# Moving the recurrence's steps and the activation blocks to other places of a fixed matmul stream

## The chip, the cores and the metric

The kernel runs on one core of one Trainium2 chip. The metric is device time in microseconds (us) of the whole program, lower is better. A core has a tensor engine (PE, with its weight loads listed as PEld), a vector engine (DVE), a scalar engine (ACT), a general engine (POOL) and a queue engine that mostly starts transfers (SP). Each executes its own list of instructions in order and waits on semaphores for the others.

## The reference, cut to what matters

One transformer-like block over 256 tokens of width 2048, all in float32:

```python
z = u @ w_in                                   # u = rms_norm(x); z is split eight ways
hq, hf, hi, hg, aq, ak, av, gates = split(z)
g = lb + (1 - lb) * sigmoid(hf); q = silu(hq) * 128**-0.5
o = hgrn2_scan(q, 1 - g, hi, log(g))           # S_t = diag(g_t) S_{t-1} + k_t v_t^T ; o_t = S_t^T q_t
y_a = rms_norm(o) * silu(hg)                   # 8 heads of 128
y_b = chunk_band_attention(aq, ak, av)         # 16 heads of 64, relative bias
merged = sig(gate_a) * (y_a @ w_branch_a) + sig(gate_b) * (y_b @ w_branch_b)
h = x + merged @ w_out
out = rms_norm(h + relu(rms_norm(h) @ w_up)**2 @ w_down)
```

## The kernel before, in words

**Products.** Every float32 product is made of three (or, transposed, two) products of split operands: a weight piece `raw` arrives by a transfer, ACT copies it into a rounded high part `wh`, DVE subtracts to get the low part `wl` (`split`, lines 88 to 90), and PE multiplies high by high, high by low and low by high. One piece is 128 x 1024. `gemm` (lines 143 to 145) spends six products of 128 x 512 on a k tile of 128 rows; `gemm_t` (lines 184 and 185) spends two pairs, each a product of 128 x 256 and one of 128 x 512. PE does little else, so its list is a stream of such products in which the rest of the work must find its place.

**The recurrence.** The scan is not run step by step. For a pair of heads, `hgrn_scores` builds a matrix of decayed scores in five steps: `diagonal` and the factors of level 2; level 2 and the factors of 8; level 8 and the factors of 32; level 32 and the factors of 128; level 128. A level step has eight short float32 products (rows named `ps`, lines 372, 416 and 448), and on DVE some exponents, products (`el`, `er`, `kl`, `qr`) and masked copies into `sd` (lines 374 and 423) that free the two `ps` buffers. `hgrn_out` then has two `outputs` steps (rows `po`, lines 476 and 477: scores times values, then a root mean square that goes ACT, DVE, POOL, DVE, ending in `o`, line 487) and two `finish` steps (rows `tpo`, line 494: transposes, then a split into `act_ya`). Four pairs of heads: pairs 0 and 1 form group 0, pairs 2 and 3 form group 1.

**What sets their order.** The steps wait in a list, `behind`. Each has a gap; `tick` takes 1 from the head's gap at each k tile of `gemm_t`, and 2 at each of `gemm`, and issues the head's step when it reaches zero. `scores(n, a, gap, first)` puts in the five score steps of pair n, `group` the eight output and finish steps of a group. The stream under them is: `hi0`, `hg0`, `hf2`, `hq2`, `hf3`, `hq3` (the input of pair 3 is `a3 = fq(3)`), `hi1`, `hg1`, `aq00`, `aq01`. What is left in the list after `aq01` is issued at once (`while behind: tick(9)`); then the pools of the stage are closed, the attention's tiles are opened in their room, and `ak00` starts. It needs the accumulator that `aq00` held, so `aq00T` (line 193) must have been read out of it; `aq00T` lies in the room of the recurrence's tiles.

**The second half.** `w_out`, `w_up` and `w_down` are done as `Unit`s: two column blocks at once, of which the first half of the k tiles uses a scheme with seven products of sums (`A`, `B`, `C`, `D`, left operands `S2`, `S4`, `S5`, `S7` that are sums of activation blocks, built by `combos`) and the second half plain products (`plain`). A unit has slots: `u.step(next(at))` is called at eleven places of `run`, numbered from 0, and issues one of the unit's waiting steps if the slot's number is at least `start`. Slot 0 lies ahead of the product `12 C`, slot 1 ahead of `11 D`, slot 2 ahead of the first plain product, slot 7 after `less("22", u2)`, the one behind the second shared copy `u2`. Besides, `plain` first issues every waiting step whose number is at most the block that it needs: at k tiles 8 and 9 that is block 2. `h_blocks` and `turns` make the steps: transposes of a block of activations (rows `tp_h`, `tp_u`, line 106), a scaling on DVE for `h` (`hw`, line 981), a split into `act_h` or `act_u`. Unit `up00` issues `h_blocks(2)`, the `dn` units whose name ends in 0 issue `turns(2)`; `wo2` issues `h_blocks(0)` and the sums of `h`; `up02`, `up12` and so on issue `turns(0)` and the sums of `u`.

The program's scheduler orders each engine's list after that, by priority and by its own notion of readiness; weight splits have high priority.

Of the kernel before, what the change touches and what calls it, by code (L numbers as in the profile page):

```python
# [50 lines left out]
def tile_hybrid_block(  # L51
# [107 lines left out]
    def later(*steps):  # L159
        behind.extend([n, f] for n, f in steps)  # L160
# [45 lines left out]
    steps = [1, 1] + [2] * (KD // 2 - 1)  # L206
# [11 lines left out]
    for kt, n in zip(starts, steps):  # L218
        c, a = kt // 4, kt % 4
        xw = h2(f"xw{kt}")[:, :n]  # L220
        nc.sync.dma_start(xw, x_t[:, kt:kt + n, :])
        with tc.high_priority(offset=2000):
            for j in range(n):
                g, hi = wmix[:, kt + j:kt + j + 1], xT[c][:, a + j, 0, :]
# [62 lines left out]
    f0, z0 = h2("f0"), h2("zq0")  # L287
# [11 lines left out]
    f1, z1 = h2("f1"), h2("zq1")  # L299
# [212 lines left out]
    def scores(n, a, gap, first=None):  # L512
        sc, steps = hgrn_scores(n, *a)
        later(*[(gap if i or first is None else first, f) for i, f in enumerate(steps)])
        return sc

    def group(g, s0, s1, vs, gws, gap):
        o0, f0 = hgrn_out(g, 0, s0, vs, gws)
        o1, f1 = hgrn_out(g, 2, s1, vs, gws)
        later(*[(gap, f) for f in o0 + o1 + f0 + f1])  # L520

    ya += [new_act(f"ya{g}") for g in range(2)]
    a0, a1 = fq(0), fq(1)
    s0 = scores(0, a0, 7, 14)
    vs0 = v_chunk(0)
    s1 = scores(1, a1, 7)
    gws0 = hg_chunk(0)
    a2 = fq(2)
    group(0, s0, s1, vs0, gws0, 4)
    a3 = fq(3)  # L530
    s2 = scores(2, a2, 7)
    vs1 = v_chunk(1)
    s3 = scores(3, a3, 7)
    gws1 = hg_chunk(1)
    group(1, s2, s3, vs1, gws1, 4)
    acc_q = [gemm_t(xT, w_in_t, C_AQ + i * T, KD, f"aq0{i}") for i in range(2)]
    while behind:
        tick(9)
# [60 lines left out]
    for g in range(2):  # L599
# [3 lines left out]
        vs = []  # L603
# [6 lines left out]
        for pr in range(5):  # L610
            last = pts
# [18 lines left out]
    def combos(lhs, what, home, made, blocks=None):  # L630

        a = {}

        def block(m, j):
            if blocks:
                a[m, j] = blocks[m, j]
                return
            a[m, j] = fours(token(f"a{m}{j}_{what}"))
            x = lhs[j][:, :, :, m * P:(m + 1) * P].bitcast(F32)
            nc.vector.tensor_tensor(a[m, j], x[:, :, 0, :], x[:, :, 1, :], op=ALU.add)  # L640

        def final(i, s):
            t = home.tile([P, 4, 2, P], F32R, name=f"S{i}_{what}", tag=f"S{i}", bufs=1)
            split(t[:, :, 0, :], t[:, :, 1, :], s)
            made[i] = [[t[:, k, u, :] for u in range(2)] for k in range(4)]

        def one():
            for m in range(NM):
                for j in range(2):
                    block(m, j)  # L650
            nc.vector.tensor_tensor(a[1, 1], a[1, 0], a[1, 1], op=ALU.subtract)
            final(5, a[1, 1])

        def two():
            nc.vector.tensor_tensor(a[1, 0], a[0, 0], a[1, 0], op=ALU.subtract)
            nc.vector.tensor_tensor(a[0, 0], a[1, 1], a[0, 0], op=ALU.subtract)
            nc.vector.tensor_tensor(a[0, 1], a[0, 1], a[0, 0], op=ALU.add)
            final(4, a[0, 1])

        return [one, two, lambda: final(2, a[0, 0]), lambda: final(7, a[1, 0])]  # L660
# [69 lines left out]
    class Unit:  # L730
# [78 lines left out]
            return half  # L809

        def step(self, at):
            if at >= self.start and self.steps:
                self.steps.pop(0)[1]()

        def end(self, n):
# [153 lines left out]
    hT = []  # L969
    Sh = {}  # L970

    def h_blocks(n0):

        def one(n, m):
            if not m:
                hT.append(new_act(f"h{n}"))
            hi, lo = hT[n][:, :, 0, :], hT[n][:, :, 1, :]
            t = h1[n][m]
            tp = transpose4(t, f"h{n}{m}")
            tmp = fours(token(f"hw_{n}_{m}"))  # L980
            nc.vector.tensor_tensor(tmp, tp, bc(wmlp[:, 4 * n:4 * n + 4], 2, P), op=ALU.mult)
            split(hi[:, :, m * P:(m + 1) * P], lo[:, :, m * P:(m + 1) * P], tmp)
            nc.scalar.activation(token(f"hsq_{n}_{m}"), t, AF.Square, accum_out=ssq2[:, m, n:n + 1])

        def factor():
            ssum2 = small.tile([P, NM], F32, name="ssum2", tag="ssum")
            nc.vector.tensor_reduce(ssum2, ssq2, axis=AX.X, op=ALU.add)
            rsqrt(rstd2, ssum2, D, NM)

        return [(n, lambda n=n, m=m: one(n, m)) for n in (n0, n0 + 1) for m in range(NM)] + [  # L990
            (n0 + 1, f) for f in ([factor] if n0 else combos(hT, "h", sp, Sh))]

    rstd2 = const.tile([P, NM], F32, name="rstd2")

# [15 lines left out]
    for qd in range(NQ):  # L1010
        last = qd == NQ - 1
        uT, rs, Su, blocks = [], {}, {}, {}

        def turns(c0, uT=uT, rs=rs, Su=Su, blocks=blocks, qd=qd):

            def one(c, m):
                if not m:
                    uT.append(new_act(f"u{qd}{c}"))
                hi, lo = uT[c][:, :, 0, :], uT[c][:, :, 1, :]
                tp = transpose4(rs[c, m], f"u{qd}{c}{m}")  # L1020
                if c < 2:
                    blocks[m, c] = fours(token(f"a{m}{c}_u{qd}"))
                    nc.scalar.copy(blocks[m, c], tp)
                split(hi[:, :, m * P:(m + 1) * P], lo[:, :, m * P:(m + 1) * P], tp)

            return [(c, lambda c=c, m=m: one(c, m)) for c in (c0, c0 + 1) for m in range(NM)] + [
                (c0 + 1, f) for f in ([] if c0 else combos(uT, f"u{qd}", tk, Su, blocks))]

        for c in range(0, 4, 2):
            def done(m, n, acc, c=c, rs=rs, qd=qd):  # L1030
                t = token(f"r{qd}{c}{n}{m}")
                with tc.high_priority(offset=2000):
                    nc.scalar.activation(t, acc, AF.Relu, scale=rstd2[:, m:m + 1])
                nc.scalar.activation(t, t, AF.Square)
                rs[c + n, m] = t

            units.append(Unit(lambda: hT, lambda: Sh, w_up, qd * (FF // NQ) + c * NC, f"up{qd}{c}", done,
                              steps=(lambda turns=turns: turns(0)) if c else (lambda: ()) if qd else (lambda: h_blocks(2)), start=3))

        def out_of(m, n, acc, last=last, qd=qd):  # L1040
            if not last:
                t = token(f"y{qd}{n}{m}")
                with tc.high_priority(offset=2000):
                    nc.scalar.copy(t, acc)
                nc.gpsimd.dma_start(hd[n][m], t, accum_op=ALU.add)
                return
            wf = fin["w"]
            r = fin[m][:, n * NC:(n + 1) * NC]
            evict(r, acc)
            nc.scalar.activation(token(f"ysq_{n}_{m}"), r, AF.Square, accum_out=ssq3[:, m, n:n + 1])  # L1050
            if n < 3:
                nc.vector.tensor_tensor(r, r, wf[:, n * NC:(n + 1) * NC], op=ALU.mult)
                return
            nc.vector.tensor_reduce(ssum3[:, m:m + 1], ssq3[:, m, :], axis=AX.X, op=ALU.add)
            rsqrt(rstd3[:, m:m + 1], ssum3[:, m:m + 1], D, 1)
            f = rstd3[:, m:m + 1]
            for i in range(4):
                t = fin[m][:, i * NC:(i + 1) * NC]
                if i == 3:
                    nc.vector.scalar_tensor_tensor(t, t, f, wf[:, i * NC:(i + 1) * NC], op0=ALU.mult, op1=ALU.mult)  # L1060
                elif i == 2:
                    nc.vector.tensor_scalar(t, t, f, None, op0=ALU.mult)
                else:
                    nc.scalar.activation(t, t, AF.Copy, scale=f)
                (nc.sync if i % 2 else nc.scalar).dma_start(out[m * P:(m + 1) * P, i * NC:(i + 1) * NC], t)

        def finals():
            fin["w"] = apool.tile([P, D], F32, name="wf", tag="act")
            nc.gpsimd.dma_start(fin["w"], bass.AP(tensor=norm_final_w.tensor, offset=norm_final_w.offset, ap=[[0, P], [1, D]]))
            for m in range(NM):  # L1070
                fin[m] = apool.tile([P, D], F32, name=f"fin{m}", tag="act")
                for n in range(4):
                    nc.gpsimd.dma_start(fin[m][:, n * NC:(n + 1) * NC], hd[n][m])

        for n0 in (0, 2):
            units.append(Unit(lambda uT=uT: uT, lambda Su=Su: Su, w_down, n0 * NC, f"dn{qd}{n0}",
                              lambda m, n, acc, n0=n0, out_of=out_of: out_of(m, n0 + n, acc), kt0=qd * KD,
                              steps=(lambda: ()) if n0 else (lambda turns=turns, last=last: turns(2) + [(3, finals)] * last),
                              start=1, tail=last and n0 == 2))

    for u, then in zip(units, units[1:] + [None]):
        run(u, then)
# [44 lines left out]
```

## Time and profile before

| | |
|---|---|
| median of 3 runs | 1416.26 us (1415.25 to 1416.26) |
| profiled execution | 1417.17 us, span 1415.4 us, mean granted clock 0.995 |
| PE busy | 1390.2 us (98%) |
| DVE busy | 1119.4 us (79%) |
| ACT busy | 908.4 us (64%) |
| POOL busy | 137.8 us (10%) |

The span runs from the first to the last instruction; the program's time is some 1.8 us longer. Times of rows count from the start of the span. A row of the timeline has its start, its duration, engine, line, operation, and the number of instructions merged in it; a bracket tells how long the engine had been idle and what ended that. Matmuls are pipelined: a product of 128 x 512 is listed with 0.39 us, and the next starts 0.23 us after it.

### The profile page before, as it was taken

To read this page: it belongs to the slowest core of one execution; us is meant where nothing else is said; L and a number is where in the kernel's file an instruction comes from. 1 tells how busy PE (TensorE), PEld (TensorE's weight loads), DVE (VectorE), ACT (ScalarE), POOL (GpSimd) and SP (SyncE) were. 2 spreads that over 40 slices of the span, in tenths; PEclk is the share of its full clock that TensorE was granted. 3 is DMA by queue.
4 is the path that set the end of the run, shared out by engine and by line. 5 is a ranking of instruction groups with operands and counts; after the bars stand their busy time and mean duration, and the time that the engine had idled before them with its cause. 6 is when DMAs were issued, how large, how long until landed. Compare 5 with 4: busy or idle time off the path is not lost.

```text
span 1415.4 us, 18570 instructions
## 1 busy us (share of the span) xinstructions
PE 1390.2 (98%) x6562; PEld 1150.4 (81%) x6562; DVE 1119.4 (79%) x1410; ACT 908.4 (64%) x1170; POOL 137.8 (10%) x220
## 2 busy tenths in 40 slices
PE   9999998999999999999999999999999999999997
PEld 7788887878787888888877888888888888888885
DVE  7897986675657875688998888779878897778885
ACT  6755744464556665445767876677666876668764
POOL 2000001010000000001210001100101001110200
PEclk9999999999999999999999999999999999999998
DMA  9644455455668987558898898988899888998883
GB/s 327 225 154 160 149 166 165 157 174 169 183 223 236 271 240 254 188 179 252 250 286 251 242 275 224 280 272 254 270 288 277 263 228 252 284 299 260 261 246 118
DMA packets 122925, 327.42 MB, mean 231 GB/s; under 512 B 10944, under 2 KB 11712, under 8 KB 122448
## 3 DMA queue, kind: packets, MB, share of 16 engines
q1 hardware_dynamic: 103264, 264.80, 54.7%
q0 software_dynamic: 18416, 59.84, 21.3%
q10 hardware_dynamic: 1152, 1.60, 0.4%
q8 instruction: 51, 0.84, 0.2%
q14 instruction: 42, 0.34, 0.1%
HBM read 271.67 MB, written 10.49 MB: 199 GB/s over the span
## 4 chain that ended last, share of the span: by engine, by line
PE 88%; DVE 4%; DMA 3%; issue 2%; ACT 2%; POOL 0%; POOLq 0%; SPq 0%; DVEq 0%; ACTq 0%
PE acc_ak L185 2%; PE acc_aq L185 2%; PE acc_hq L185 2%; PE acc_hf L185 2%; PE ps L416 1%; PE acc_aq L184 1%; PE acc_ga L144 1%; PE acc_ga L145 1%; PE acc_av L144 1%; PE acc_ga L143 1%; PE acc_ba L143 1%; PE acc_ba L145 1%; PE acc_av L145 1%; PE acc_av L143 1%; PE acc_ba L144 1%
## 5 line engine op out<-in xcount | busy, mean ns | idle before, releaser
L185 PE MATMUL acc_ak<-act_x,wh_ak 128*128 128x512 f32 x128 | 46.2, 405 | 1.8 <-DVE aq00T L193 1.8
L185 PE MATMUL acc_aq<-act_x,wh_aq 128*128 128x512 f32 x128 | 46.3, 400 | 0.0
L185 PE MATMUL acc_hq<-act_x,wh_hq 128*128 128x512 f32 x128 | 46.2, 398 | 0.0
L185 PE MATMUL acc_hf<-act_x,wh_hf 128*128 128x512 f32 x128 | 45.9, 396 | 0.0
L90 DVE TENSOR_TENSOR wl_ga<-raw_ga,wh_ga 128x1024 fp32r<-128x1024 f32 x16 | 19.6, 1225 | 19.6 <-ACT wh_ga L89 19.6
L184 PE MATMUL acc_aq<-act_x,wl_aq 128*128 128x256 f32 x120 | 35.0, 292 | 0.0
L184 PE MATMUL acc_hf<-act_x,wl_hf 128*128 128x256 f32 x120 | 34.4, 287 | 0.2 <-DVE wl_hf L90 0.2
L184 PE MATMUL acc_hq<-act_x,wl_hq 128*128 128x256 f32 x120 | 34.2, 285 | 0.0
L184 PE MATMUL acc_ak<-act_x,wl_ak 128*128 128x256 f32 x120 | 34.0, 283 | 0.0
L90 DVE TENSOR_TENSOR wl_av<-raw_av,wh_av 128x1024 fp32r<-128x1024 f32 x16 | 19.6, 1224 | 17.5 <-ACT wh_av L89 17.5
L89 ACT CAST wh_bb<-raw_bb 128x1024 fp32r<-128x1024 f32 x16 | 16.9, 1054 | 23.3 <-PE acc_ba L145 17.7
L90 DVE TENSOR_TENSOR wl_aq<-raw_aq,wh_aq 128x1024 fp32r<-128x1024 f32 x16 | 19.6, 1224 | 15.1 <-ACT wh_aq L89 15.1
L89 ACT CAST wh_ak<-raw_ak 128x1024 fp32r<-128x1024 f32 x16 | 16.8, 1050 | 22.7 <-PE acc_ak L185 11.5
L90 DVE TENSOR_TENSOR wl_bb<-raw_bb,wh_bb 128x1024 fp32r<-128x1024 f32 x16 | 19.6, 1223 | 14.8 <-ACT wh_bb L89 14.8
L89 ACT CAST wh_av<-raw_av 128x1024 fp32r<-128x1024 f32 x16 | 16.8, 1052 | 21.9 <-PE acc_av L145 12.4
L89 ACT CAST wh_aq<-raw_aq 128x1024 fp32r<-128x1024 f32 x16 | 16.8, 1049 | 21.8 <-PE acc_hg L145 9.2
L185 PEld LDWEIGHTS acc_ak<-act_x,wh_ak 128*128 128x128 f32 x128 | 24.6, 193 | 7.5 <-DVE aq00T L193 2.0
L89 ACT CAST wh_ba<-raw_ba 128x1024 fp32r<-128x1024 f32 x16 | 16.8, 1053 | 20.8 <-PE acc_bb L145 13.8
L89 ACT CAST wh_hg<-raw_hg 128x1024 fp32r<-128x1024 f32 x16 | 16.8, 1050 | 20.8 <-PE acc_hg L145 12.6
L90 DVE TENSOR_TENSOR wl_ba<-raw_ba,wh_ba 128x1024 fp32r<-128x1024 f32 x16 | 19.6, 1223 | 12.5 <-ACT wh_ba L89 12.5
L185 PEld LDWEIGHTS acc_aq<-act_x,wh_aq 128*128 128x128 f32 x128 | 24.0, 188 | 5.4 <-issue 0.7
L185 PEld LDWEIGHTS acc_hq<-act_x,wh_hq 128*128 128x128 f32 x128 | 24.1, 188 | 5.3
(1807 smaller groups left out, 5254.8 us busy)
## 6 DMA issues: line engine op xcount, KB each, us to landing
raw_hi<-in_w_in_n_dram SPq DMA_DIRECT2D x16, 512.0 KB, 4.2
raw_hg<-in_w_in_n_dram SPq DMA_DIRECT2D x16, 512.0 KB, 3.8
raw_aq<-in_w_in_t_dram SPq DMA_DIRECT2D x16, 512.0 KB, 4.0
raw_ak<-in_w_in_t_dram SPq DMA_DIRECT2D x16, 512.0 KB, 3.8
raw_av<-in_w_in_n_dram SPq DMA_DIRECT2D x16, 512.0 KB, 4.2
raw_ga<-in_w_in_t_dram SPq DMA_DIRECT2D x16, 512.0 KB, 4.6
raw_ba<-in_w_branch_a_dram SPq DMA_DIRECT2D x16, 512.0 KB, 4.6
raw_bb<-in_w_branch_b_dram SPq DMA_DIRECT2D x16, 512.0 KB, 4.6
```

The costliest lines, as they stand in the source:

```text
L89: (copy or nc.scalar.copy)(hi, src)
L90: nc.vector.tensor_tensor(lo, src, hi.bitcast(F32), op=ALU.subtract)
L143: nc.tensor.matmul(acc, hi, wh, start=first, stop=False, skip_group_check=True)
L144: nc.tensor.matmul(acc, hi, wl, start=False, stop=False, skip_group_check=True)
L145: nc.tensor.matmul(acc, lo, wh, start=False, stop=last, skip_group_check=True)
L184: nc.tensor.matmul(acc[:, cb, 0:T], wl[:, c], r[:, 0, :], start=False, stop=False)
L185: nc.tensor.matmul(acc[:, cb, :], wh[:, c], r.rearrange("p u t -> p (u t)"), start=kt == 0, stop=kt == nkt - 1)
L416: nc.tensor.matmul(ps[:, m, :], klf[:, a * P:(a + 1) * P], qrf[:, a * 192:(a + 1) * 192], start=True, stop=True)
```

## The change

Three edits. First, the recurrence's steps get other gaps, and the five score steps of pair 2 are put in the list ahead of `a3 = fq(3)` rather than behind it; outputs and finishes have gaps of their own. Second, steps may carry a slot of their own as a third entry: the sums of activations (`combos`) and the reduction of `h`'s squares (`factor`) carry 7. Third, the units that begin by turning blocks they need themselves (`up00` and the `dn` units whose name ends in 0) have `start` 0 in place of 3 and 1.

```diff
-    def group(g, s0, s1, vs, gws, gap):
+    def group(g, s0, s1, vs, gws, gap, gap2):
         o0, f0 = hgrn_out(g, 0, s0, vs, gws)
         o1, f1 = hgrn_out(g, 2, s1, vs, gws)
-        later(*[(gap, f) for f in o0 + o1 + f0 + f1])
+        later(*[(gap, f) for f in o0 + o1], *[(gap2, f) for f in f0 + f1])
...
-    s0 = scores(0, a0, 7, 14)
+    s0 = scores(0, a0, 8, 20)
     vs0 = v_chunk(0)
-    s1 = scores(1, a1, 7)
+    s1 = scores(1, a1, 8)
     gws0 = hg_chunk(0)
     a2 = fq(2)
-    group(0, s0, s1, vs0, gws0, 4)
+    group(0, s0, s1, vs0, gws0, 3, 4)
+    s2 = scores(2, a2, 6)
     a3 = fq(3)
-    s2 = scores(2, a2, 7)
     vs1 = v_chunk(1)
-    s3 = scores(3, a3, 7)
+    s3 = scores(3, a3, 6)
     gws1 = hg_chunk(1)
-    group(1, s2, s3, vs1, gws1, 4)
+    group(1, s2, s3, vs1, gws1, 2, 3)
...
         def step(self, at):
-            if at >= self.start and self.steps:
+            if self.steps and at >= (self.steps[0][2] if len(self.steps[0]) > 2 else self.start):
                 self.steps.pop(0)[1]()
...
-            (n0 + 1, f) for f in ([factor] if n0 else combos(hT, "h", sp, Sh))]
+            (n0 + 1, f, 7) for f in ([factor] if n0 else combos(hT, "h", sp, Sh))]
...
-                (c0 + 1, f) for f in ([] if c0 else combos(uT, f"u{qd}", tk, Su, blocks))]
+                (c0 + 1, f, 7) for f in ([] if c0 else combos(uT, f"u{qd}", tk, Su, blocks))]
...
-                              steps=(...) if c else (lambda: ()) if qd else (lambda: h_blocks(2)), start=3))
+                              steps=(...) if c else (lambda: ()) if qd else (lambda: h_blocks(2)), start=3 if c else 0))
...
-                              start=1, tail=last and n0 == 2))
+                              start=0, tail=last and n0 == 2))
```

More of the change, by code (lines that the diff above doesn't have):

```diff
@@ L1037, in tile_hybrid_block @@
             units.append(Unit(lambda: hT, lambda: Sh, w_up, qd * (FF // NQ) + c * NC, f"up{qd}{c}", done,
-                              steps=(lambda turns=turns: turns(0)) if c else (lambda: ()) if qd else (lambda: h_blocks(2)), start=3))
+                              steps=(lambda turns=turns: turns(0)) if c else (lambda: ()) if qd else (lambda: h_blocks(2)), start=3 if c else 0))
         def out_of(m, n, acc, last=last, qd=qd):
```

## The prediction

> **What bounds the kernel now.** The page's busy times and the chain that ended last come first: PE is the bound, and a change that adds or drops no product can only move PE's waits.
>
> ```profile
> PE 1390.2 (98%) x6562; PEld 1150.4 (81%) x6562; DVE 1119.4 (79%) x1410; ACT 908.4 (64%) x1170; POOL 137.8 (10%) x220
> ...
> PE 88%; DVE 4%; DMA 3%; issue 2%; ACT 2%; POOL 0%; POOLq 0%; SPq 0%; DVEq 0%; ACTq 0%
> ```
>
> Next the list of PE's waits: who waited, for whom, us in total, times, longest.
>
> ```profile
> PE tpo L494 <- DVE act_ya L90: 2.3, 1, 2.3
> PE acc_wo2c L143 <- ACT u_wo L756: 2.1, 1, 2.1
> PE ps L416 <- DVE qr L405: 1.9, 2, 1.7
> PE acc_ak L185 <- DVE aq00T L193: 1.8, 1, 1.8
> ...
> PE po L477 <- DVE o L487: 1.1, 1, 1.1
> ...
> PE acc_up00c L143 <- ACT act_h L89: 1.0, 1, 1.0
> ...
> PE ps L372 <- DVE q L338: 0.5, 1, 0.5
> ...
> PE tp_h L106 <- DVE hw L981: 0.4, 2, 0.3
> ...
> PE acc_dn30c L144 <- DVE wl_dn30r L90: 0.2, 1, 0.2
> ```
>
> All but `wo2c` (2.1) lie where a step moves. Third, the busy times by stage: the stretch, PE, PEld, DVE, ACT, POOL (counts in brackets), the granted clock, the share of the transfers, GB/s.
>
> ```profile
> 162.00:195.00 33.00, 33.00 (x157) 28.20 (x157) 32.13 (x78) 21.43 (x29) 0.00 (x0) 1.00 0.49 157
> 195.00:216.00 21.00, 21.00 (x102) 18.04 (x102) 13.94 (x35) 6.83 (x7) 0.00 (x0) 1.00 0.53 168
> ...
> 245.00:250.00 5.00, 3.10 (x12) 2.44 (x13) 4.40 (x10) 1.63 (x4) 0.72 (x4) 0.75 0.67 181
> ...
> 715.00:720.00 5.00, 5.00 (x16) 3.91 (x15) 3.80 (x5) 3.33 (x5) 0.00 (x0) 0.66 1.03 411
> ...
> 725.00:750.00 25.00, 23.79 (x112) 19.19 (x111) 24.71 (x27) 17.20 (x23) 4.85 (x7) 1.00 1.02 270
> ```
>
> DVE is full beside `hi1` (32.13 of 33 us) and in the unit `up00` (24.71 of 25), so what moves there may only change who waits. And twice, behind a wait of 2 us, the granted clock falls: 0.75 and 0.66 over 5 us.
>
> **The change, part by part.** What moves is read from the lists of instructions of both built kernels, whose order is fixed; the durations are the rows'.
>
> *The end of the recurrence.* Before, four finishes are left behind `aq01` and issued in one go.
>
> ```profile
> 241.99 0.40 PE L185 MATMUL acc_aq<-act_x,wh_aq 128*128 128x512 f32 x1
> 242.23 0.60 PE L494 MATMUL tpo<-ident,o 128*128 128x128 f32 x4
> 245.12 0.77 PE L494 MATMUL tpo<-ident,o 128*128 128x128 f32 x4 [2.29 <-DVE act_ya L90]
> 247.68 0.80 PE L185 MATMUL acc_ak<-act_x,wh_ak 128*128 128x512 f32 x1 [1.79 <-DVE aq00T L193]
> ...
> 250.97 0.28 PE L184 MATMUL acc_ak<-act_x,wl_ak 128*128 128x256 f32 x1
> ...
> 246.94 0.68 DVE L193 TENSOR_TENSOR aq00T<-acc_aq,aq00T 128x512 f32<-128x512 f32 x1
> ...
> 151.34 0.28 PE L184 MATMUL acc_hq<-act_x,wl_hq 128*128 128x256 f32 x1
> ...
> 151.69 0.28 PE L184 MATMUL acc_hq<-act_x,wl_hq 128*128 128x256 f32 x1
> ...
> 152.05 0.38 PE L494 MATMUL tpo<-ident,o 128*128 128x128 f32 x2
> ...
> 152.62 0.28 PE L184 MATMUL acc_hq<-act_x,wl_hq 128*128 128x256 f32 x1
> ```
>
> In the new list the last finish stands 12 products into `aq01`, with 52 behind it (26 pairs x 0.35 us, 151.34 to 151.69, = 9.1 us), and DVE and ACT read `aq00T` out beside it. Both waits then end long before `ak00` is reached. From 242.23 to 250.97, where `ak00` is back at speed, 8.74 us pass. They hold 5 pairs of `ak00` (1.75 us), and four finishes, which placed singly cost 0.23 us each (151.69 to 152.62 is 0.93, two pairs are 0.70): 0.92. Gain 8.74 - 1.75 - 0.92 = **6.1 us**. 4.08 of it are the two waits, 1.65 the slow clock behind them (3.29 us from 247.68 for products that take 1.75), the rest the pipeline's turns. At least 2.3 goes if only the finishes' own wait ends; 6.1 is the most.
>
> Here the Trainium skill ("TensorE: Matmul & The Clock Gate", Part 1) says that PE's clock goes to half after an idle window of some 3.4 us, windows running free of the kernel. By it neither wait is long enough, the slow products would have another cause, and the part would be worth 4.5 us. The rows side against that length: the wait of 2.05 us ahead of `wo2c` alone was followed by 0.66.
>
> *Pair 0's scores* start 13 products of `hi0` later and have 24, not 19, ahead of level 2.
>
> ```profile
> 62.70 0.39 PE L144 MATMUL acc_hi<-wl_hi,act_x 128*128 128x512 f32 x1
> ...
> 69.09 0.39 PE L145 MATMUL acc_hi<-wh_hi,act_x 128*128 128x512 f32 x1
> ...
> 71.16 1.54 PE L416 MATMUL ps<-qr,kl 128*128 128x192 f32 x8 [1.68 <-DVE qr L405]
> ...
> 67.27 0.55 ACT L389 ACTIVATE er<-er 128x384 f32<-128x384 f32 x1
> ...
> 68.16 1.28 ACT L332 ACT_TABLE_LOAD   x1
> ...
> 69.46 0.63 ACT L332 ACTIVATE sq<-zq 128x512 f32<-128x512 f32 x1
> ...
> 70.73 0.28 DVE L405 TENSOR_TENSOR qr<-qr,rr 128x128 f32<-128x128 f32 x1
> 71.05 1.23 DVE L90 TENSOR_TENSOR wl_hi<-raw_hi,wh_hi 128x1024 fp32r<-128x1024 f32 x1
> ```
>
> The first wait (0.5) goes. PE reaches level 2 at 62.70 + 14 x 0.23 + 1.3 for the diagonal + 24 x 0.23 = about 72.7. But `qr` moved back too. After `er` (67.7) ACT now casts `hi0_14` (1.05), then loads tables and does `sq` (1.3 + 0.6, 70.6), loads again and does `rr` (72.1), then casts `hg0_0` (73.2). On DVE that piece's low part (1.14) now stands ahead of the last `qr`, which ends near 74.6. A wait of 1.9 takes the place of 1.7 + 0.5: gain **0.3**, between 2.2 (all gone) and -1.3 (the clock falls).
>
> *Group 0's outputs* reach the third `po` after 44 products of `hf3`, as before; what it waits for, ACT's and DVE's chain through `o`, keeps its order. The 1.1 stays; the fourth comes two products (0.35) sooner and one finish (0.23) later, and so waits a little more: loss **0.1**, bounds 0 and 0.5.
>
> *Pairs 2 and 3.* The scores of 2 begin at `hi1`'s first product, not 18 later, and have 18 between levels, not 24.
>
> ```profile
> 166.10 1.28 ACT L322 ACT_TABLE_LOAD   x1
> 167.39 0.63 ACT L322 ACTIVATE lg<-f 128x512 f32<-128x512 f32 x1
> ...
> 168.06 1.23 DVE L324 TENSOR_TENSOR_SCAN b<-reset,lg 128x512 f32<-128x512 f32 x1 [0.59 <-ACT lg L322]
> ```
>
> The mask copies that free the diagonal's buffers now stand on DVE behind this scan, which waits for `lg`; one cast of ACT's is moved behind `lg`, which so comes some 1.3 us sooner; the scan ends near 167.8, and the first buffer is free at 168.0. PE is there at 162.06 + 1.3 + 18 x 0.23 = 167.5: a wait of 0.5, and the level's two halves are split by one product (0.15). From there each level takes 18 x 0.23 + 1.3 = 5.4 us of PE; DVE's share, one and a half low parts at 1.14 and 2.5 to 3.6 us of the step's own, is 4.2 to 5.3. It just holds. Over the stretch DVE did 32.13 + 13.94 = 46.1 of 54 us; two level steps that were beside `aq00` come in (about 5), so 51 of 54. Loss **0.65**, bounds 0 and 11 (second rival). Group 1's outputs, 8 products apart, run into `aq00`; the chain behind `hg1` (gate, `o`) is just done when the fourth `po` wants its buffer: loss **0.15**, bounds 0 and 1.1, the row of group 0.
>
> *Needed blocks from slot 0.* In `up00` block 2's transposes move from ahead of the plain product that needs them to slots 0 and 1, block 3's to slot 2 and the plain.
>
> ```profile
> 739.90 1.28 DVE L90 TENSOR_TENSOR S_h<-a_h,S_h 128x512 fp32r<-128x512 f32 x2
> ```
>
> From 741.1 DVE in its new order has S7 (0.6), a low part (1.14), `hw` (0.6), three low parts, then `act_h` at 747.5; ACT's half is ready near 746.4, when PE gets there. The second half comes near 750.5, some 0.3 late, and the last transposes find their buffer 0.1 late. So 0.4 stands for 1.2 (1.0, and 0.2 of `tp_h`): gain **0.75**, bounds 1.2 and, since DVE is full and a `hw` may hold up a low part, -0.7. In the four `dn` units the turns move up one slot. There PE waited 0.2 in all, and the activations that slot 0 and 2 turn are squared before: 0, bounds 0.2 and, per unit, -0.3, `tp_h`'s longest. `finals` moves up a slot as well, POOL's list is the same: 0. On SP one load of `up02` changes places with another: 0, as casts wait for PE there.
>
> *Sums behind slot 7.* Nothing moves: `plain` at k tiles 8 and 9 issues all steps numbered up to block 2 ahead of slot 3, and the sums carry 1. Only `factor` moves, a reduction that is due at the unit's end: 0. Had it worked, the 2.1 ahead of `wo2c` and its 0.66 could have gone; they stay.
>
> *Sum*: -6.1 - 0.3 + 0.1 + 0.65 + 0.15 - 0.75 = -6.25 us. The profiled execution's 1417.17 becomes 1410.9; it was 0.9 above the median, and 1416.26 becomes **1410.0**.
>
> **The rivals.** *Less comes free.* The release of the recurrence's room, not the order, holds `aq00T`, or DVE's lag passes into `aq01`; then only the finishes' own wait goes. For it: DVE is at 51 of 54 us. Against it: 9.1 us of cover. -2.3 + 0.6 - 0.75 leaves about 1413.8.
>
> *Slower.* DVE becomes the bound in `hi1` and `hg1`. Each of the eight level steps of pairs 2 and 3 has 6 x 0.23 = 1.4 us less of cover. If DVE's list, full between 162 and 195 already, can't shrink, PE waits that much at each: 11 us against 6.1, so 1416.26 - 6.25 + 11 = 1421. It decides from a DVE step of 5.4 us on; losses pass the gain once they exceed 0.8 a step. For it speaks 32.13 of 33, against it the 13.94 of 21 behind.
>
> *The clock's phase.* A wait near 2 us may or may not draw the slow clock. If the wait of 1.9 in `hi0` does, add 1.65: 1411.7. If the one in `wo2`, 6 us earlier now, no longer does: 1408.4. The rows show 1.7 without a fall and 2.05 with one. The Trainium skill's free-running window (same page and part) would make that a matter of phase; no run here shows it yet.
>
> **How the numbers follow.** Forecast 0.55 (1408.8 to 1411.3 by itself); clock lost 0.10, clock won 0.07; less comes free 0.15; slower 0.10; a loss that just cancels the gain 0.03. The range from 1407.8 to 1414.8 holds the first four and cuts off the slower ones. 0.2% of 1416, 2.8 us, is about what a measurement tells from no change: faster are the forecast and both clock cases with a little of the fourth, 0.75; within it the rest of the fourth and the cancelling, 0.15; slower 0.10.
>
> **What would show it.** Right: no row `tpo` with four transposes ahead of `ak00`, no wait of `acc_ak` for `aq00T`, granted clock 1.0 from 245 on; a wait of about 1.9 at the first level 2; waits on `ps` under 1 us beside `hi1`; under 0.5 in `up00`; `wo2c` unchanged. Wrong: waits of over 1 us at several `ps` rows between 160 and 215, or low parts of weights that PE waits for there.

## The result, and the profile after

The changed kernel takes 1410.2 us (median of 6 runs, 1409.62 to 1411.39) against 1415.92 for the kernel before in the same series (1414.95 to 1417.19). The ratio is 0.9961 (95% interval 0.9948 to 0.9974): 5.5 us less, 3.7 to 7.4. The forecast was 1410.0. Its profiled execution took 1411.28 us with a span of 1409.5, against 1417.17 and 1415.4: 5.9 us less, where the sum of the forecast was 6.25.

The page of the changed kernel, its busy times and the chain that ended last:

```profile
PE 1387.3 (98%) x6562; PEld 1149.8 (82%) x6562; DVE 1119.1 (79%) x1410; ACT 909.0 (64%) x1170; POOL 137.0 (10%) x220
...
PE 93%; DVE 3%; ACT 2%; issue 1%; DMA 0%; POOL 0%; SPq 0%; POOLq 0%; DVEq 0%; ACTq 0%
```

The work is the same. Of the 2.9 us that went from PE's busy time some 1.6 are products that had run at a slow clock (two slow stretches before, one now); the rest was not traced. Next, PE's list of waits in the changed kernel:

```profile
PE ps L416 <- DVE qr L405: 2.2, 1, 2.2
PE acc_wo2c L143 <- ACT u_wo L756: 2.1, 1, 2.1
...
PE po L477 <- DVE o L487: 1.1, 1, 1.1
...
PE tp_h L106 <- DVE hw L981: 0.8, 1, 0.8
...
PE ps L416 <- DVE sd L374: 0.7, 1, 0.7
PE acc_wo0c L144 <- DVE wl_wo0r L90: 0.5, 1, 0.5
PE po L476 <- DVE ms L95: 0.3, 1, 0.3
```

`tpo`, `acc_ak` and `acc_up00c` are gone. New are the whole of the 2.2 at the first level 2 (1.7 and 0.5 before), the 0.7 beside `hi1`, and two small ones in `wo0` and `wo2`. The stages of the changed kernel (columns as in the prediction), with the granted clock in the third column from the right:

```profile
76.00:80.00 4.00, 4.00 (x14) 3.25 (x13) 3.08 (x9) 0.73 (x1) 0.00 (x0) 0.62 0.64 227
162.00:195.00 33.00, 32.31 (x156) 27.37 (x155) 32.24 (x76) 22.05 (x32) 0.00 (x0) 1.00 0.47 152
195.00:216.00 21.00, 21.00 (x104) 18.15 (x103) 15.30 (x42) 6.25 (x8) 0.00 (x0) 1.00 0.46 149
245.00:250.00 5.00, 5.00 (x30) 4.33 (x29) 5.00 (x8) 3.50 (x5) 0.00 (x0) 1.00 0.46 137
712.00:717.00 5.00, 5.00 (x23) 4.12 (x23) 5.00 (x6) 4.77 (x7) 0.00 (x0) 1.00 1.02 367
725.00:750.00 25.00, 25.00 (x118) 20.29 (x118) 24.22 (x30) 17.81 (x26) 3.81 (x6) 1.00 1.00 290
```

The gap at 245 is filled (5.00 of 5, 30 instructions where there were 12), `up00` is full. The slow clock has moved: it stands behind the wait in `hi0` (0.62), and not behind the one in `wo2`, which is as long as before. The rows, in the timeline of the changed kernel:

```profile
74.71 1.99 PE L416 MATMUL ps<-qr,kl 128*128 128x192 f32 x8 [2.16 <-DVE qr L405]
76.25 0.88 PE L143 MATMUL acc_hi<-wh_hi,act_x 128*128 128x512 f32 x1
76.93 0.63 PE L144 MATMUL acc_hi<-wl_hi,act_x 128*128 128x512 f32 x1
77.35 0.63 PE L145 MATMUL acc_hi<-wh_hi,act_x 128*128 128x512 f32 x1
...
168.88 0.89 PE L416 MATMUL ps<-qr,kl 128*128 128x192 f32 x4 [0.69 <-DVE sd L374]
...
235.98 0.38 PE L494 MATMUL tpo<-ident,o 128*128 128x128 f32 x2
...
245.38 0.40 PE L185 MATMUL acc_ak<-act_x,wh_ak 128*128 128x512 f32 x1
245.61 0.28 PE L188 MATMUL acc_ak<-act_x,wl_ak 128*128 128x256 f32 x1
...
711.77 0.50 PE L143 MATMUL acc_wo2c<-wh_wo2r,act_m 128*128 128x512 f32 x1 [2.05 <-ACT u_wo L756]
712.11 0.39 PE L144 MATMUL acc_wo2c<-wl_wo2r,act_m 128*128 128x512 f32 x1
```

Where PE does the same products in both kernels, the starts of the same row give the running account, changed minus before: -0.25 us at 60 (first weight pieces, ahead of anything that was edited), +0.4 at 134, -3.5 from 270 to 686, -2.7 and -2.15 behind the two new waits in `wo0` and `wo2`, -3.8 behind the slow stretch that `wo2` no longer had, -5.3 behind `up00`, -5.9 at the end.

### The profile page after: what moved, and what is told of

Its sections match the earlier page's. It is cut to its first block, busy times and chain, and to the rows that moved or that the text cites. A ratio compares the mean times of both kernels' runs of the same rounds, so it can differ in the third digit from the quotient of the medians.

```text
span 1409.5 us, 18582 instructions
## 1 busy us (share of the span) xinstructions
PE 1387.3 (98%) x6562; PEld 1149.8 (82%) x6562; DVE 1119.1 (79%) x1410; ACT 909.0 (64%) x1170; POOL 137.0 (10%) x220
## 4 chain that ended last, share of the span: by engine, by line
PE 93%; DVE 3%; ACT 2%; issue 1%; DMA 0%; POOL 0%; SPq 0%; POOLq 0%; DVEq 0%; ACTq 0%
PE acc_ak L185 2%; PE acc_hq L185 2%; PE acc_aq L185 2%; PE acc_hf L185 2%; PE ps L416 1%; PE tp_u L106 1%; PE acc_ga L144 1%; PE acc_hg L144 1%; PE acc_hg L145 1%; PE acc_hg L143 1%; PE acc_ga L145 1%; PE acc_bb L143 1%; PE acc_ga L143 1%; PE acc_ba L143 1%; PE acc_av L145 1%; PE acc_ba L145 1%
## 5 line engine op out<-in xcount | busy, mean ns | idle before, releaser
L185 PEld LDWEIGHTS acc_hf<-act_x,wh_hf 128*128 128x128 f32 x128 | 24.1, 188 | 5.3 <-DVE f L193 0.3
```

Source lines behind the costliest of these rows:

```text
L185: nc.tensor.matmul(acc[:, cb, :], wh[:, c], r.rearrange("p u t -> p (u t)"), start=kt == 0, stop=kt == nkt - 1)
```

## The experiments

**The end of the recurrence alone.** On top of the kernel before (with `gap2` in `group`, as in the change):

```diff
-    group(1, s2, s3, vs1, gws1, 4)
+    group(1, s2, s3, vs1, gws1, 2, 2)
```

> The kernel before with one thing changed: group 1's outputs and finishes 2 k tiles apart, not 4, so that the four last finishes are issued in aq01 (8 products apart, 12 behind the last) and nothing is left for the loop behind it. Theory (the forecast's first term): both waits and the slow clock behind them go, 6.1 us, less 0.2 to 0.6 for group 1's outputs being closer together: 5.5 to 5.9 faster than before, a ratio of 0.996, and no row of four transposes ahead of ak00. Rival, only the finishes' own wait goes and aq00T is late still: 2.3 us, 0.9984. Rival by the Trainium skill's clock rule (TensorE: Matmul & The Clock Gate, Part 1), the slow products have another cause and stay: 4.5 us, 0.9968.

Measured: 1411.1 against 1417.37, ratio 0.996 (0.9947 to 0.9972). From its timeline the rows ahead of `ak00`, and from its stages the granted clock there (1.00):

```profile
241.59 0.38 PE L494 MATMUL tpo<-ident,o 128*128 128x128 f32 x2
244.06 0.50 PE L185 MATMUL acc_ak<-act_x,wh_ak 128*128 128x512 f32 x1
244.40 0.28 PE L188 MATMUL acc_ak<-act_x,wl_ak 128*128 128x256 f32 x1
```

```profile
240.00:245.00 5.00, 5.00 (x31) 4.17 (x30) 4.50 (x8) 3.06 (x6) 1.77 (x4) 1.00 0.67 174
```

No wait for `aq00T`, although only 12 products stand behind the last finish, and no slow clock. By the starts of rows, from +0.35 at 225 us to -4.9 at 270, this version gained 5.2 us, net of what the closer outputs cost. The rival of 2.3 is out by both readings. The other, 4.5, lies inside the interval that the times allow (4.0 to 7.5 us), near its end, but does not fit the profile: the slow products behind the two waits went with the waits.

**The blocks alone.** On top of the kernel before, the `start` edits only (3 to 0 in `up00`, 1 to 0 in `dn`).

> The kernel before with only the third edit (needed blocks from slot 0). Forecast: 0.75 us faster in up00 and nothing in the dn units, ratio 0.9995. By the changed kernel's starts of rows it is more: 1.7 in up00 (743.06 to 748.69 holds 1.66 us more than its products take, though the rows name 1.2 of waits) and 0.1 to 0.4 in each dn unit's 200 us: 2.0 to 2.3 in all, 0.9985. Rival: in the changed kernel up00 gained since the recurrence's edits had moved the transfers against PE; then the third edit alone gives 0 to 0.75.

Measured: 1415.99 against 1417.37, ratio 0.9992 (0.9983 to 1.0001). By starts of rows `up00` gained 1.5 (from -1.25 ahead of it to -2.8 behind), as in the changed kernel (-3.8 to -5.3), and the `dn` units 0.2 to 0.3 together. So the recurrence's edits have no part in it. The times give 1.1 (-0.1 to 2.4), which holds this and the forecast's 0.75 as well; that it is 1.5 rests on the traces. It is more than the waits that went, and the timeline of the kernel before shows why:

```profile
746.44 0.39 PE L145 MATMUL acc_up00c<-wh_up00p21A,S_h 128*128 128x512 f32 x1
746.99 0.66 PE L106 MATMUL tp_h<-ident,h 128*128 128x128 f32 x4 [0.16 <-DVE hw L981]
748.69 0.50 PE L143 MATMUL acc_up00c<-wh_up00r,act_h 128*128 128x512 f32 x1 [1.05 <-ACT act_h L89]
749.03 0.39 PE L144 MATMUL acc_up00c<-wl_up00r,act_h 128*128 128x512 f32 x1
749.26 0.60 PE L106 MATMUL tp_h<-ident,h 128*128 128x128 f32 x4
749.62 0.71 PE L143 MATMUL acc_up00c<-wh_up00r,act_h 128*128 128x512 f32 x2
```

From the product at 746.44 to the next but one at 749.03 pass 2.59 us; two products (0.46) and a set of transposes (0.36, 749.26 to 749.62) take 0.82. So 1.77 went by, where the brackets say 1.21. A bracket begins at the listed end of the last product. The 0.16 by which that end lies behind the place where the next product would have started (0.39 listed, 0.23 from start to start), and some 0.1 at the restart, belong to the wait too.

**Pair 0's and 1's scores back at their old places**, on top of the changed kernel:

```diff
-    s0 = scores(0, a0, 8, 20)
+    s0 = scores(0, a0, 7, 14)
...
-    s1 = scores(1, a1, 8)
+    s1 = scores(1, a1, 7)
```

> The changed kernel with pair 0's and 1's scores back at their old places (first 14, gap 7). Theory: the 2.16 us wait in hi0 and the slow clock behind it (4.3 us lost by the starts of rows between 60 and 80, 2.9 before) come from the later start, so this version is 1.4 us faster than the changed one: ratio to before 0.995, waits of 0.5 and 1.7 at the first two ps rows and a clock of 1.0 from 75 to 100. Rival, the slow clock behind a wait of 2 us is a matter of chance in each execution: on average only 0.3 slower to 0.6 faster than the changed kernel, 0.9957 to 0.9963. Rival, the steps behind (level 2 to 128 of pair 0 and 1) lose in hg0 what hi0 wins: the same as the changed kernel.

Measured: 1410.25 against 1417.37, ratio 0.9955 (0.9943 to 0.9968). The profile has the waits of the kernel before again (0.48, 1.70, and 0.2 at level 8 in `hg0`) and no slow clock; from 134 on it stands 0.65 us ahead of the changed kernel, not 1.4. The excess that the theory took from the rows up to 80 was incomplete: the old places lose again in `hg0`, as the last rival had it in part. The times can't tell the two kernels apart.

**The second edit, made to work.** On top of the changed kernel, `plain` leaves alone the steps that carry a slot:

```diff
-            while self.steps and self.steps[0][0] <= ks[-1] // 4:
+            while self.steps and len(self.steps[0]) == 2 and self.steps[0][0] <= ks[-1] // 4:
```

> The changed kernel with the second edit made to work: plain no longer issues steps that carry a slot of their own, so the sums wait for slot 7 and the ones behind. Theory: the 2.05 us wait ahead of wo2c comes from the cast S_h on ACT, which waits 3.8 us for DVE's sum a_h with the copy u_wo behind it; with the sums moved it goes, and its slow clock where there was one: 2.3 to 2.6 us faster than the changed kernel, ratio to before 0.9943, and in the four up units whose name ends in 2 nothing. Rival: the sums are then late for the next unit's second product (comb 5), 1 us in each of five units: 2.5 slower than the changed kernel, 0.998. Rival: DVE is full there in any order (24.8 of 25 us) and another row waits instead: the same as the changed kernel, 0.996.

Measured: 1414.02 against 1417.37, ratio 0.9979 (0.997 to 0.9988): some 2.5 us slower than the changed kernel. The wait ahead of `wo2c` at slot 7 did go, as the theory had it. Then this, in PE's timeline, in the stage around it, and in the waits of ACT and of DVE from 706 to 742:

```profile
727.51 0.80 PE L144 MATMUL acc_wo2c<-wl_wo2r,act_m 128*128 128x512 f32 x1 [2.60 <-DVE wl_wo2r L90]
...
734.25 0.50 PE L144 MATMUL acc_up00c<-wl_up00p11D,act_h 128*128 128x512 f32 x1 [0.76 <-DVE wl_up00p11D L90]
```

```profile
727.00:732.00 5.00, 4.49 (x14) 3.62 (x15) 4.67 (x6) 0.12 (x1) 0.54 (x1) 0.66 1.01 323
```

```profile
ACT wh_wo2r L89 <- DMA rawp_wo2r<-in_w_out_dram: 4.8, 1, 4.8
```

```profile
DVE wl_wo2r L90 <- ACT wh_wo2r L89: 3.5, 1, 3.5
```

Without that wait PE came 2.4 us sooner, by the starts of rows, to pieces that were not there yet: ACT waited 4.8 us for a transfer, and DVE 3.5 for ACT, with moved sums (`a_h`) behind that low part in its list. From there on DVE was busy without a gap until PE waited 2.6 us for another low part, with a slow clock again (0.66). The time was taken back, and more, in `up00`.

**The sums of `h` alone, together at slot 7.** As before, but the sums of `u` carry no slot, and `step` issues all of those of `h` at slot 7.

> The changed kernel with the sums of h, and they alone, kept out of plain and all issued at slot 7 (they were spread over slots 7 to 10 in the version before, with the sums of u too). If that version lost since its sums were late for up00, this one wins what the wait ahead of wo2c is worth, 2.1 to 2.5 us: 0.9945. If it lost since the pieces rawp_wo2r come no sooner (ACT waited 4.76 us for that transfer) and DVE has the sums beside up00's low parts in any order, this one loses about as much: 0.9975 to 0.998, with a wait of 2 to 3 us for a low part wl_wo2r.

Measured: 1414.7 against 1416.92, ratio 0.9984 (0.9975 to 0.9994), a wait of 2.15 us for `wl_wo2r` at 729.78 and the same small ones in `up00`. So the second of its two cases: how the sums are spread is not the cause. Which share the late transfer has and which DVE's full list, these two runs don't separate.

**The price of a wait by itself.** In front of the kernel before stand 56 bursts of 36 to 48 products, each ended by a chain on DVE of one of eight lengths.

> The kernel before with 56 bursts of 36 to 48 products ahead of everything else (8 to 11 us each at 0.23), with a chain of DVE between each two that lets PE wait, in eight lengths from about 1 to about 3 us, seven times each. It is for the price of a wait alone: how often are the products behind a wait at half speed (0.43 in place of 0.23 us from start to start), and for how long, by the length of the wait? The time of the program means nothing here. The Trainium skill's rule as written (TensorE: Matmul & The Clock Gate, Part 1: an idle window of some 3.4 us): none behind any wait of less than 3.4. A fixed threshold near 2: none below it, all above. Chance by phase (the case's own rows: 1.7 none in three executions, 2.05 to 2.16 in five of eight): none below about 1.7, a share that grows with the length from there on, nearly all at 3.

Three of its bursts in the timeline (all products are equal, 0.227 us each at full speed, which with 0.16 more for the listed end of the last makes 10.2, 8.3 and 10.6), and the stage in which the third begins:

```profile
117.41 10.27 PE L94 MATMUL ps_wide<-wide 128*128 128x512 f32 x44 [1.63 <-DVE wide L98]
129.81 8.45 PE L94 MATMUL ps_wide<-wide 128*128 128x512 f32 x36 [2.13 <-DVE wide L98]
...
152.30 12.31 PE L94 MATMUL ps_wide<-wide 128*128 128x512 f32 x46 [1.80 <-DVE wide L98]
```

```profile
152.00:156.00 4.00, 3.70 (x10) 2.90 (x11) 0.24 (x1) 0.00 (x0) 0.00 (x0) 0.59 0.00 0
```

The third is longer by 1.7, with a clock of 0.59 at its start, behind a shorter wait than the second's. Of the 49 waits that stand clear of other work:

```
wait (us)        1.47  1.63  1.80  1.96  2.13  2.30  2.47  2.63
bursts              6     6     7     5     6     7     6     6
slowed              0     0     4     3     2     4     4     5
```

A slowed burst took 1.45 to 1.65 us longer than the others (one 2.9). Neither a full window of idle time nor a threshold near 2 fits; a chance that begins between 1.63 and 1.80 does. That it grows from there (13 of 25 up to 2.30, 9 of 12 above) is not clear with so few bursts.

What decides is in the trace's own record of the granted clock. It is 0.50 for stretches of 3.41 us (one of twice that) and 1.00 around them; here is the one of the third burst, between its neighbours:

```profile
149.29:152.70 3.41, 1.61 (x8) 1.03 (x7) 1.57 (x5) 0.00 (x0) 0.00 (x0) 1.00 0.00 0
152.71:156.12 3.41, 3.41 (x10) 2.65 (x9) 0.00 (x0) 0.00 (x0) 0.00 (x0) 0.50 0.00 0
156.13:159.53 3.40, 3.40 (x17) 2.80 (x16) 0.00 (x0) 0.00 (x0) 0.00 (x0) 1.00 0.02 5
```

The 23 slow stretches among the bursts all begin on one grid of 3.4133 us, to within 0.001. Every window of this grid in which PE idled for more than 1.85 us was followed by half clock, no window with less than 1.79, and four of the seven in between; only the second half of the double stretch (0.67 of idle ahead of it) stays unexplained. So the clock is set window by window, and a wait counts by how much of it falls into one window: its length gives the chance, its place on the grid decides. The kernels' own traces have the same grid. The two slow stretches of one execution begin 137.0 windows apart in the kernel before (247.46 and 715.09), and 191.0 apart in both versions with moved sums.

**The changed kernel, profiled twice more.**

> The changed kernel unchanged, for a second profiled execution. Both waits of about 2 us stay as long as they were (2.16 at the first level 2 in hi0, 2.05 ahead of wo2c), since they are set by the lists. If what draws the slow clock is the place in the program, hi0 has it (granted clock near 0.62 from 76 to 80) and wo2 has not (1.00 from 710 to 722), as in the first. If it is the phase of a window of 3.4 us that runs free, in which PE must idle for 1.7 or more, each wait has it in about 6 executions of 10 (at 2.05: 1.35 + 0.7 of 3.4), whatever it did in the first.

> The changed kernel unchanged, for a third profiled execution: as the second. By the place in the program: hi0 slow, wo2 not. By a free window: each in about 6 of 10, so that three executions agree at both places in about 1 case of 13.

The waits were 2.17 and 2.15 in `hi0`, 2.06 and 2.05 in `wo2`. The clock, in the second execution and then in the third:

```profile
76.00:80.00 4.00, 4.00 (x12) 3.13 (x12) 3.15 (x10) 1.27 (x2) 0.00 (x0) 0.57 0.60 222
710.00:714.00 4.00, 3.61 (x10) 2.80 (x11) 3.70 (x5) 3.32 (x5) 0.00 (x0) 0.61 1.03 412
```

```profile
76.00:80.00 4.00, 4.00 (x15) 3.50 (x15) 3.16 (x9) 0.72 (x1) 0.00 (x0) 0.74 0.60 218
710.00:718.00 8.00, 6.49 (x21) 5.18 (x22) 7.01 (x9) 6.47 (x10) 0.00 (x0) 0.79 1.02 393
```

`wo2` was slow in both, and was not in the first: the same program, the same wait. The place in the program does not decide. The slow stretches in `hi0` and `wo2` begin 186.0 windows of 3.4133 us apart in the second execution and 187.0 in the third. Divided by that length from the start of the span, the beginning of `hi0`'s stretch leaves 0.56, 0.91 and 2.98 us in the three executions: the grid runs free of the program. In the first execution a boundary of the grid that `hi0`'s stretch fixes cuts the wait in `wo2` into 0.82 and 1.23 us, and neither part is enough; the 13 slow stretches behind such waits in the kernels' traces all follow a window with 1.97 us of idle or more. `hi0` was slow all three times, and also in the two versions with moved sums, whose waits there are 2.14 and 2.17. Five of five is what a chance of 0.6 gives in one case of thirteen, so a higher chance at that place is not ruled out; the wait of 2.05 in `wo2` was slow in four of the eight executions that have it. Single spans were 1409.5, 1409.6 and 1410.7; the two new waits of the first execution in `wo0` and `wo2` (0.5 and 0.8) were 0 and 0.5, then 0.2 and 0.9, so they too come and go with the transfers there.

**Level 2 later.** The version that the readings point to: on top of the changed kernel, the two `ps` waits are removed by giving the steps gaps one by one.

```diff
-        later(*[(gap if i or first is None else first, f) for i, f in enumerate(steps)])
+        later(*zip(gap, steps))
...
-    s0 = scores(0, a0, 8, 20)
+    s0 = scores(0, a0, (20, 12, 7, 7, 6))
...
-    s2 = scores(2, a2, 6)
+    s2 = scores(2, a2, (6, 8, 6, 6, 6))
```

(`s1` and `s3` keep 8 and 6 throughout.)

> The changed kernel with pair 0's level 2 four ticks (12 products, 2.75 us) later and the steps behind it a tick closer together, and pair 2's level 2 two ticks (6 products, 1.4 us) later. Theory (both waits are PE's being too early for DVE's chain, whose order stays): the 2.16 us in hi0 with its slow clock, 4.3 us by the starts of rows, and the 0.7 (1.0 by starts) beside hi1 go; group 1's steps stand 2 ticks later: 4 to 5 us faster than the changed kernel, ratio to before 0.9925 to 0.993. Rival: DVE's list is full and passes the wait to the next rows (level 8 in hg0, the low parts): 1 to 2 us, 0.9945 to 0.9955. Rival: nothing, 0.996, if the end is set by the transfers at 700 to 735.

Measured: 1406.02 against 1416.92, ratio 0.9924 (0.991 to 0.9938), the fastest version here. The rows:

```profile
75.67 1.46 PE L416 MATMUL ps<-qr,kl 128*128 128x192 f32 x8
...
165.74 1.46 PE L416 MATMUL ps<-qr,kl 128*128 128x192 f32 x8
```

Neither has a bracket. Against the changed kernel its rows stand 0.55 us later at 60, 3.6 earlier at 134, 4.7 earlier at 188 and 4.8 at the end; about 1.65 of this is the slow stretch in `hi0`, which it does not have. In the recurrence DVE passed nothing on, and the transfers at 700 to 735 did not hold the end; in `up00` a wait of 0.6 for a sum `S_h` is new.

## Why the prediction was right, and where by luck

*The end of the recurrence* (6.1, with group 1's outputs at -0.15: 5.95 net). Shown, at 5.2: so much the version with that part alone gained. In the changed kernel the account from 60 to 270 is -3.25; with 0.65 lost by pair 0 and 1 (+0.4 at 134, from -0.25), 0.15 by group 0 and 1.1 by pairs 2 and 3 (what the later level 2 brought back) the rest is again some 5.2. Of the 0.75 that is missing, some 0.35 are group 1's outputs: two `po` rows start 0.23 and 0.28 late, where 0.15 was forecast. The other 0.4 was not placed. The 1.65 that the working gives the slow clock is 1.54 by the rows beside it (3.29 less 1.75); the 6.1 does not use it, and the rival built on it would stand at 4.55 rather than 4.5. The rule of the Trainium skill ("TensorE: Matmul & The Clock Gate", Part 1) that was weighed there, half clock behind an idle window of some 3.4 us, put the part at 4.5. The measurements differ from it: waits of 1.80 already did it in four of seven bursts, so the slow products at 247 belonged to the waits, as the forecast took it. That its windows run free of the kernel, and their length, agree with the clock's record above (3.4133 us).

*Pair 0's scores* (+0.3). The wait was forecast at 1.9 and is 2.16, in place of 1.68 and 0.48; the chain behind `qr` was read right. The part lost 0.65. The step that failed is its value, taken without the slow clock, which the working had only in its lower bound of -1.3. All three executions of the changed kernel had it, at some 1.65 each; without it the part would have won 1.0, as the brackets undervalue the waits that went. "The rows show 1.7 without a fall and 2.05 with one" should have given this rival far more than 0.10.

*Group 0's outputs* (-0.1): the third `po` waits 1.1 again; by the starts up to 161, where both kernels have done the group, 0.15 is lost.

*Pairs 2 and 3* (-0.65). The wait at `ps` for the masked copies `sd` is 0.69 where 0.5 was forecast; from start to start it costs 0.85 and the split halves 0.14, and 1.1 came back when level 2 was moved. The mechanism is right; the term is short by what the bracket leaves out and by 0.2 of the wait's length. "It just holds" held: no other `ps` row waits, DVE is at 32.24 + 15.30 = 47.5 of 54 us where 51 was forecast, and the slower rival is out.

*Needed blocks from slot 0* (+0.75). 1.5. Two errors of one sign: 0.4 of waits was forecast to stay and none did, and the 1.2 that went was read from brackets, which hid some 0.55 behind the last product and at the restart. For the `dn` units 0 was forecast; 0.2 to 0.3 came in the version with that edit alone.

*Sums behind slot 7* (0). Confirmed by the traces: from `wo0` on, the changed kernel and the version with the blocks alone, which lacks the second edit, run the same instructions in the same order on all five engines (3408 products and transposes on PE). But the remark that with a working edit "the 2.1 ahead of `wo2c` and its 0.66 could have gone" was half of the story. The wait went, and the next limit took back more.

*The total.* From -6.25 to the -5.9 of the profiled execution: +0.75 at the end of the recurrence, +1.0 in pair 0, +0.05 in group 0, +0.45 in pairs 2 and 3, against -0.75 in `up00`, -0.5 behind it, -0.25 ahead of 60, and -0.3 in `wo0` and `wo2`, where the clock's luck (-1.65) met two new waits (+1.4). That gives -5.8; the 0.1 that is left lies within the rounding of these terms. Both cases of the rival "the clock's phase" came true at once in that execution, and their effects cancelled. That the time came out within 0.2 us of the forecast is luck in that sense: the forecast of the time was better than that of its parts.

## What to carry to other kernels

Take the price of a wait from the starts of the rows around it, not from the bracket: with products of 0.23 us from start to start each wait here cost 0.15 to 0.3 us more than it is listed with. A PE wait between 1.8 and 2.6 us may cost another 1.6 us or not, by chance, so it is worth most to bring waits of 2 us below 1.6, even by making a step later; here 12 products of delay were worth some 4 us, the slow stretch included. And before a wait is removed, look at what PE will then reach sooner: in a stage with transfers at 1.0 and DVE at 24 of 25 us it may only meet the next one.

## What was not expected of the hardware

Waits of 1.80 us were followed by half clock in 4 of 7 cases, waits of 1.63 in 0 of 6; the same wait of 2.05 in the same program was followed by it in two executions and not in a third. Behind this stands a grid of windows of 3.4133 us that runs free of the program: in the test with bursts half clock lasted for whole windows of it, and followed a window when PE had idled in it for more than about 1.8 us. A single profile therefore carries about 1.6 us of chance for each wait of that size.
